# PSUM in eight one-bank tiles read by halves, sums of tile pairs copied from bank to bank, and a held-back channel sum in a Hymba-style layer

## The chip, the cores and the metric

The kernel runs on one core of a Trainium2 chip. The time is the device time of one execution in microseconds; the number that counts is the median over several runs.

## What is computed

One layer works on x of 1024 tokens and 1024 channels. Cut to what matters:

```python
h = rmsnorm(x, norm_g) * (1 + scale) + shift          # shift, scale, gate = silu(c) @ mod_w + mod_b
cv, cg, cs, lx, ls = split(h @ w_in)                  # five times 1024 channels
v = cv * sigmoid(cg)
v = causal_depthwise_conv(v, dw_w, dw_b)              # 31 taps
v = silu(layernorm(v, cln_g, cln_b))                  # over the channels
y_conv = (v @ pw2_w + pw2_b) * silu(cs)
xs = causal_depthwise_conv(lx, sc_w, sc_b)            # 4 taps
r = sigmoid(per head: xs @ wr + br); i = sigmoid(per head: xs @ wi + bi)
log_a = -8 * r * softplus(-lam)
hs = scan: h_t = exp(log_a) h_(t-1) + sqrt(1 - exp(2 log_a)) * (i * xs)
y_lru = hs * silu(ls)
x = x + (1 + gate) * (concat(y_conv, y_lru) @ w_out)
return rmsnorm(x, final_g)
```

## The kernel before

Everything is held with channels on 128 partitions and the 1024 tokens (T) along the free dimension; H is 512, half of them. A product in full precision is made of three matmuls: both operands are split into a high and a low part (`whi`, `wlo`; `uh`, `ul`), and high by high, high by low and low by high are added in PSUM. ScalarE casts the high part (L325), VectorE or GpSimd subtracts to get the low one (L352).

The work runs in this order. A first group of tiles, then 36 tiles `ps4` to `ps39` of the input projection (`mm_k`, L468: for each k both column halves), in the order of the list ORDER. Between them stand eight gates of the RG-LRU (`gates`, L1148): 12 matmuls each on `xsh`, `xsl`, the split result of the short convolution `xs`, with a low part that VectorE makes last. What is done with a finished tile is in `evac_in` (L1106): sigmoid, product, silu, short convolution. The 31-tap convolution is done on VectorE in two one-bank PSUM sums `cacc`, `caccs` for five of the eight channel tiles; for tiles 1, 3 and 5 ScalarE makes the products (`cq`, `co`) and DMAs issued by GpSimd add them up (`es`, `oo`). When a convolution is done, `c0` to `c7` are added up in `csum` (`conv_sum`, L1084): seven adds, the first six on GpSimd and the last on VectorE, in the order of SUMS, each when its operand is there.

Then come the tiles `ps40` to `ps47` of the output projection on the lru half. In between, the layer norm (L1178): the mean by a matmul on `csum` (L1184), subtractions, squares, their sums (L673), a spread of the inverse deviation over the partitions (`lnbc`, L679), multiplications, silu. Then `pw2` in four pairs of tiles and the conv half of the output projection: tile 6 on its own (`out`, L651), three pairs, tile 7. A pair (`pair_products`, L576 to L645) uses seven products of Strassen's scheme as Winograd wrote it (L590), 12 matmuls of 128x512 each, on sums of weight quarters (`rawpw`, `rawout`, split to `h12`, `l12`, `h34`, `l34`) and sums of token and channel quarters (`T1` to `T4`, `vt`, `vu`, `yt`, `yu`). Two two-bank tiles `pa`, `pb` take the products; ScalarE copies `pa` to SBUF (`e`), VectorE adds `pb` to it (`epw`, `eout`), and the readers take the sum of `e` and the rest of the tile. At the end stands the final norm by column pieces (`norm`, L1341) and the stores, issued by SyncE (L376) and ScalarE.

The order on each engine is fixed before the run by the class Plan: every operation has an engine, an estimated cost and a priority (n is the number of the tile in the order), operations it depends on, and buffers; a list scheduler picks for each engine the operation with the lowest priority that is ready in its model. Buffers come from pools (47 of [128, 1024] in SBUF; in PSUM three tiles of two banks and two of one); the next user of a buffer waits for the last reader of the one before. Each engine works through its own queue in that fixed order, so an operation that waits holds up all that stand behind it on its engine. DMAs are issued from the queues of SyncE, GpSimd and ScalarE.

Of the kernel before, what the change touches and what calls it, by code (L numbers as in the profile page):

```python
# [9 lines left out]
F32 = mybir.dt.float32  # L10
# [38 lines left out]
QGATES = ((2, 5), (3, 0), (3, 2), (3, 2))  # L49
OUT_A, OUT_P, OUT_Z = (6,), (0, 1, 2), (7,)  # L50
# [6 lines left out]
SUMS = (2, 6, 1, 4, 3, 0, 5, 7)  # L57
# [42 lines left out]
class Plan:  # L100
# [23 lines left out]
    def op(self, eng, cost, emit, prio, r=(), w=(), table=None, after=(), reserve=0,  # L124
# [28 lines left out]
        o.psum = [(b, any(k[0] is b for k in w)) for b in o.bufs if b.pool in ("mm", "acc")]  # L153
# [127 lines left out]
def hymba_layer(ctx: ExitStack, tc: tile.TileContext, xT, vecs, mod_w, w_first, w_in,  # L281
# [10 lines left out]
    psum = ctx.enter_context(tc.tile_pool(name="psum", bufs=3, space=bass.MemoryType.PSUM))  # L292
    psacc = ctx.enter_context(tc.tile_pool(name="psacc", bufs=2, space=bass.MemoryType.PSUM))
# [7 lines left out]
    pools["mm"] = (psum, "mm", [P, T], 3)  # L301
    pools["acc"] = (psacc, "acc", [P, H], 2)
# [35 lines left out]
    def in_psum(r):  # L338
        return any((k[0] if isinstance(k, tuple) else k).pool in ("mm", "acc") for k in r
                   if isinstance(k[0] if isinstance(k, tuple) else k, Buf))  # L340
# [39 lines left out]

    def part(b, a, e):
        return lambda: b()[:, a:e]

    def halves(b, a, e):
        return [(b, i) for i in range(b.parts) if i * (T // b.parts) < e
                and a < (i + 1) * (T // b.parts)]
# [75 lines left out]
    def mm_k(prio, ps, s, xh, xl, k, cols, off=0, nk=KT, after=()):  # L462
        wh, wl = whi[s], wlo[s]

        def emit():
            for lhs, rhs, last in ((wh, xh, 0), (wh, xl, 0), (wl, xh, 1)):
                for a, b in cols:
                    pe.matmul(ps()[:, a - off:b - off], k3(lhs)()[:, k, :], rhs[k]()[:, a:b],  # L468
                              start=(k == 0 and lhs is wh and rhs is xh
                                     and (a - off) % H == 0),  # L470
                              stop=(k == nk - 1 and bool(last)), skip_group_check=True)
# [9 lines left out]

    def mm_tile(name, parts=2):
        return S.buf("mm", name, F32, parts)

    def acc_tile(name):
        return S.buf("acc", name, F32)

# [88 lines left out]
    def pair_products(name, n, w, sets, apart=0, plain=False):  # L576

        pa, pb = (S.buf("mm", f"p{z}{name}", F32) for z in "ab")
# [3 lines left out]
        def product(q, a, b, ps, start):  # L585
            (wh, wl), xs = w[a], sets[b]
            for j, (bh, bl) in enumerate(xs):
                def emit(j=j, bh=bh, bl=bl):
                    for lhs, rhs, z in ((wh, bh, 0), (wh, bl, 1), (wl, bh, 2)):
# [4 lines left out]
                         [ps[0]], columns=3 * H)  # L594
                if j == 0:
                    ops.append(o)
        product(0, "A11", "B11", (pa, 0), True)
        if plain:
            pc = acc_tile(f"pc{name}")
            ACT(pr, half(e, 0), half(pa, 0), "copy", H, r=[pa], w=[(e, 0)])  # L600
            product(1, "S4", "B22", (pc, 0), True)
            product(2, "A12", "B21", (pa, 0), False)
            product(3, "S1", "T1", (pa, 1), True)
            ACT(pr, half(e, 1), half(pa, 1), "copy", H, r=[pa], w=[(e, 1)])
            product(4, "S2", "T2", (pb, 0), True)
            product(5, "S3", "T3", (pb, 1), True)
            TT(pr, "DVE", e, e, pb, ALU.add, r=[e, pb], w=[e])
            product(6, "A22", "T4", (pb, 1), False)
            yield ops, e, {(0, 0): (half(pa, 0), pa), (0, 2): (pc, pc),
                           (1, 1): (half(e, 1), (e, 1)), (0, 1): (half(pa, 1), pa),  # L610
                           (1, 0): (half(pb, 1), pb)}
            return
        if apart:
            ACT(pr, half(e, 0), half(pa, 0), "copy", H, r=[pa], w=[(e, 0)])
            f = big_buf(f"f{name}")
        else:
            product(1, "S1", "T1", (pa, 1), True)
            ACT(pr, e, pa, "copy", r=[pa], w=[e])
        product(2, "S2", "T2", (pb, 0), True)
        product(3, "S3", "T3", (pb, 1), True)  # L620
        if apart:
            TT(pr, "DVE", half(e, 0), half(e, 0), half(pb, 0), ALU.add, H, r=[(e, 0), pb],
               w=[(e, 0)])
            ACT(pr, part(f, 0, H), half(pb, 1), "copy", H, r=[pb], w=[f])
        else:
            TT(pr, "DVE", e, e, pb, ALU.add, r=[e, pb], w=[e])
        product(4, "A12", "B21", (pa, 0), False)
        if apart:
            product(5, "A22", "T4", (pb, 1), False)
            yield ops, e, {(0, 0): (half(pa, 0), pa), (1, 0): (half(pb, 1), pb)}  # L630
            n += apart
            product(6, "S1", "T1", (pa, 1), True)
            ACT(pr, half(e, 1), half(pa, 1), "copy", H, r=[pa], w=[(e, 1)])
            TT(pr, "DVE", half(e, 1), half(e, 1), part(f, 0, H), ALU.add, H, r=[(e, 1), f],
               w=[(e, 1)])
            product(7, "S4", "B22", (pa, 1), False)
            yield ops, e, {(1, 1): (half(e, 1), (e, 1)), (0, 1): (half(pa, 1), pa)}
            return
        product(5, "S4", "B22", (pa, 1), False)
        product(6, "A22", "T4", (pb, 1), False)  # L640
        yield ops, e, {(0, 0): (half(pa, 0), pa), (1, 1): (half(e, 1), (e, 1)),
                       (0, 1): (half(pa, 1), pa), (1, 0): (half(pb, 1), pb)}

    def tail_mm(prio, ps, off, s, sets, k, a, e):
# [4 lines left out]
        def emit():  # L649
            for lhs, (rhs, i), last in ((wh, (bh, ih), 0), (wh, (bl, il), 0), (wl, (bh, ih), 1)):  # L650
                pe.matmul(ps()[:, a - off:e - off], k3(lhs)()[:, k, :],  # L651
# [8 lines left out]
    def rstd(prio, sqs, a, e, ps, o, after=(), warm=(), idle=None):  # L660
# [4 lines left out]
        wk = halves(ps, o, o + e - a)  # L665
# [5 lines left out]
        def stats(sq, k):  # L671
            for b in range(nb):
                pe.matmul(ps()[:, o + b:o + b + 1], sq()[:, a + b * P:a + b * P + P],  # L673
# [3 lines left out]
        def spread(ps=ps):  # L677
            for b in range(nb):
                pe.matmul(ps()[:, o + b * P:o + b * P + P],  # L679
                          rs()[:, b:b + 1].to_broadcast([P, P]), ident, start=True, stop=True)  # L680
# [5 lines left out]
        ACT(prio, lambda: sd()[:, :nb], lambda: ps()[:, o:o + nb], AF.Sqrt, nb, bias=eps_t,  # L686
# [13 lines left out]
    psf = [mm_tile(f"first{n}", 4) for n in range(3)] + [acc_tile("first3")]  # L700
    psb = acc_tile("token_stats")
# [4 lines left out]
    cs, ps_c = ctile("cs", KT), [mm_tile(f"c_row{z}") for z in (0, 1)]  # L706
# [29 lines left out]
    def fw_mm(prio, ps, i, xh, xl, k, cols, after=(), off=0, z=None):  # L736
# [5 lines left out]
        def emit():  # L742
            for lhs, rhs, last in terms:
                for a, b in cols:
                    pe.matmul(ps()[:, a - off:b - off], fw_part(lhs, k, i * P, i * P + P)(),  # L745
# [174 lines left out]
    psx = mm_tile("psbias", 2)  # L920
# [52 lines left out]
    def by_two(b, a, e):  # L973
        return lambda: b()[:, a:e].rearrange("p (m q) -> p q m", q=2)
# [22 lines left out]
    def conv_tile(i):  # L997
# [19 lines left out]
        if i in POOLED:  # L1017
# [6 lines left out]
        acc, acs = acc_tile(f"cacc{i}"), acc_tile(f"caccs{i}")  # L1024
        acc_e, acc_s = half(acc, 0), half(acs, 0)
        ACT(pr, acc_e, ev, AF.Identity, H, scale=w(0), bias=vec("dw_b", i), r=[vi, ("V", 1)],
            w=[acc], after=held[-1:])
        o = ACT(pr, acc_s, src_s, AF.Identity, H, scale=ws(0), bias=b2,
            r=[(ci, 0), ("V", 1), ("wsum", 0)], w=[acs])
        held.append(o)  # L1030
# [7 lines left out]
        TT(pr, "DVE", every(1), every(1), acc_e, ALU.subtract, H, r=[ci, acc], w=[ci])  # L1038
        ACT(pr, acc_s, od, AF.Copy, H, scale=w(1), r=[vi], w=[acs])
        for r in range(1, 15):  # L1040
# [3 lines left out]
        TT(pr, "DVE", cut(every(0), 1, H), cut(every(0), 1, H), cut(acc_s, 0, H - 1), ALU.add,  # L1044
           H - 1, r=[ci, acs], w=[ci])
# [59 lines left out]
    def evac_in(m, ps, n, b=None, rb=()):  # L1105
        pr = n + 0.5  # L1106
        kind, i = (m // KT) * KT, m % KT
        if kind == CG:
            sig[i] = big_buf(f"sig{i}")
            ACT(pr, sig[i], ps, AF.Sigmoid, r=[ps], w=[sig[i]])  # L1110
        elif kind == CV:
            sg = sig.pop(i)
            v[i] = big_buf(f"v{i}")
            TT(pr, "DVE", apart(v[i], 0, T), by_two(ps, 0, T), by_two(sg, 0, T), ALU.mult,
               r=[ps, sg], w=[v[i]])
        elif kind == CS:
            t = big_buf(f"scs{i}")
            ACT(pr, t, ps, AF.Silu, bias=b, r=[ps, *rb], w=[t])
            scs_d[i] = dram.tile([P, T], F32, tag=f"scs{i}", name=f"scsd{i}")
            DMA(pr, lambda: scs_d[i], t, FULL_BYTES, r=[t], w=[("scsd", i)])  # L1120
        elif kind == LS:
            sls[i] = big_buf(f"sls{i}")
            ACT(pr, sls[i], ps, AF.Silu, bias=b, r=[ps, *rb], w=[sls[i]])
        else:
# [6 lines left out]
            ACT(pr, xs, ps, AF.Identity, scale=w(0), bias=vec("sc_b", i), r=[ps], w=[xs])  # L1131
            for s in range(1, STAPS):
                STT(pr, part(xs, s, T), part(ps, 0, T - s), w(s), part(xs, s, T), ALU.mult,
                    ALU.add, T - s, r=[ps, xs], w=[xs])
# [3 lines left out]
    def gates(i, n):  # L1138
# [3 lines left out]
        for j, (dst, b) in enumerate(((r, "br"), (g, "bi"))):  # L1142
            ps = mm_tile(f"gate{i}_{j}")

            def emit(j=j, ps=ps):
                for lhs, rhs, st in ((hi, xh, 0), (hi, xl, 1), (lo, xh, 2)):
                    for c0, c1 in FULL:
                        pe.matmul(ps()[:, c0:c1], lhs()[:, j, :], rhs()[:, c0:c1],  # L1148
                                  start=st == 0, stop=st == 2)
            S.op("PE", 6 * 0.2267, emit, n + 0.01 * j, [hi, lo, xh, xl], [ps],  # L1150
                 columns=6 * H)
            ACT(n + 0.2, dst, ps, AF.Sigmoid, bias=vec(b, i), r=[ps], w=[dst])
# [25 lines left out]
    def layer_norm():  # L1178
        pr = 45
        mean = mm_tile("mean")  # L1180
# [282 lines left out]
```

## Time and profile before

| | |
|---|---|
| median of 3 runs | 744.27 us (743.26 to 744.53) |
| the profiled execution | 745.16 us |
| its span, first to last instruction | 743.3 us |
| TensorE busy, mean granted clock | 731.4 us (98%), 0.996 |
| VectorE busy | 630.0 us (85%) |
| ScalarE busy | 446.8 us (60%) |
| GpSimd busy | 157.7 us (21%) |

The time of the profiled execution holds 1.9 us outside its span. PE is TensorE's matmuls, PEld its weight loads, DVE is VectorE, ACT ScalarE, POOL GpSimd and SP SyncE. Rows of the chain and of the timeline give the start in us from the span's start, the length, the engine, the line and the tile; rows of groups give the busy time, the mean ns of one instruction, and the idle time ahead of them with what ended it. Rows of the windows give for each engine its busy time and the number of its instructions, then the granted TensorE clock, the busy share of the DMA engines and their GB/s.

### The profile page before, as it was taken

The page shows a single profiled execution, that of the slowest core. Times are in us where ns is not written, and L with a number is a line of the kernel's source. Part 1 is how long each engine was busy: PE and PEld are TensorE (multiplying, and loading weights), DVE is VectorE, ACT ScalarE, POOL GpSimd, SP SyncE. Part 2 cuts the span into 40 slices and gives each one's busy share as a digit, 9 for nine tenths or more (in the row PEclk, how much of TensorE's full clock was granted, in tenths as well). Part 3 has the DMA queues.
Part 4 walks back from the last instruction along what each step waited for, and adds up shares of the span by engine and source line. Part 5 has one row for each costly group of instructions (what it writes and reads, how often), then busy time and mean ns, then how long its engine had stood idle before and what let it go on. Part 6 is the DMA issues. An engine that isn't in the chain of part 4 may idle for free.

```text
span 743.3 us, 8920 instructions
## 1 busy us (share of the span) xinstructions
PE 731.4 (98%) x3314; PEld 607.4 (82%) x3314; DVE 630.0 (85%) x818; ACT 446.8 (60%) x560; POOL 157.7 (21%) x137
## 2 busy tenths in 40 slices
PE   9999999999999999999998999999999999999996
PEld 8888888887888888888887888878888888877886
DVE  6998999896899886887899868886998766999945
ACT  6650587758877969937838685734843224455422
POOL 0033022462443433432272110400000000000003
PEclk9999999999999999999999999999999999999999
DMA  9961025586899799699483445252433530623206
GB/s 335 407 217 57 0 100 121 140 171 148 183 244 242 144 220 229 144 223 195 106 169 70 116 97 167 74 181 102 155 113 98 187 113 1 223 73 126 88 1 227
DMA packets 37052, 111.59 MB, mean 150 GB/s; under 512 B 4112, under 2 KB 12816, under 8 KB 37008
## 3 DMA queue, kind: packets, MB, share of 16 engines
q1 hardware_dynamic: 23616, 75.97, 29.3%
q0 software_dynamic: 12528, 34.26, 25.4%
q10 hardware_dynamic: 864, 0.79, 0.3%
q8 instruction: 26, 0.43, 0.2%
q14 instruction: 18, 0.15, 0.1%
HBM read 64.16 MB, written 12.58 MB: 103 GB/s over the span
## 4 chain that ended last, share of the span: by engine, by line
PE 83%; DVE 12%; ACT 2%; issue 2%; DMA 1%; SPq 0%; DVEq 0%; ACTq 0%
PE ps L468 59%; PE first L745 5%; PE papw L590 4%; PE pbpw L590 3%; PE gate L1148 3%; PE pbout L590 2%; PE paout L590 2%; PE out L651 2%; DVE wlo L352 1%; DMA fraw<-in_w_first_dram 1%; DVE xs L344 1%; DVE fin L344 1%; PE late L745 1%; DVE yu L352 1%; DVE rawout L352 1%
## 5 line engine op out<-in xcount | busy, mean ns | idle before, releaser
L468 PE MATMUL ps<-uh,whi 128*128 128x512 f32 x576 | 177.5, 389 | 0.6 <-ACT sls L333 0.6
L468 PE MATMUL ps<-uh,wlo 128*128 128x512 f32 x576 | 177.8, 390 | 0.0
L468 PE MATMUL ps<-ul,whi 128*128 128x512 f32 x576 | 177.7, 390 | 0.0
L468 PEld LDWEIGHTS ps<-uh,whi 128*128 128x128 f32 x576 | 108.0, 188 | 23.4 <-ACT sls L333 1.1
L468 PEld LDWEIGHTS ps<-uh,wlo 128*128 128x128 f32 x576 | 108.4, 188 | 22.6
L468 PEld LDWEIGHTS ps<-ul,whi 128*128 128x128 f32 x576 | 108.2, 188 | 22.4
L325 ACT CAST whi<-raw 128x1024 fp32r<-128x1024 f32 x46 | 48.1, 1048 | 50.2 <-PE ps L468 34.9
L352 POOL TENSOR_TENSOR o<-fin,bc 128x256 f32<-128x256 f32 (+1 forms) x8 | 7.3, 945 | 259.2 <-ACT bc L325 259.2
L357 POOL DMA_DIRECT2D es<-cq x45 | 40.7, 913 | 99.0 <-ACT cq L333 68.6
L333 ACT ACT_TABLE_LOAD x45 | 57.7, 1283 | 4.4 <-DVE sp8h L366 2.9
L352 DVE TENSOR_TENSOR wlo<-raw,whi 128x1024 fp32r<-128x1024 f32 x36 | 49.3, 1371 | 8.4 <-ACT whi L325 8.3
L344 DVE SCALAR_TENSOR_TENSOR cacc<-v,V,cacc 128x511 f32<-128x511 f32 (+14 forms) x75 | 55.5, 740 | 0.2
L357 POOL DMA_DIRECT2D oo<-co x42 | 40.8, 1016 | 59.8 <-ACT co L333 23.6
L344 DVE SCALAR_TENSOR_TENSOR caccs<-v,V,caccs 128x511 f32<-128x511 f32 (+6 forms) x70 | 52.1, 744 | 1.3
L344 DVE SCALAR_TENSOR_TENSOR caccs<-c,wsum,caccs 128x511 f32<-128x511 f32 (+6 forms) x70 | 52.0, 742 | 0.7
L352 POOL TENSOR_TENSOR wlo<-raw,whi 128x1024 fp32r<-128x1024 f32 x10 | 24.9, 2501 | 111.6 <-ACT whi L325 111.6
L468 PE MATMUL ps<-yh,whi 128*128 128x512 f32 x128 | 40.0, 394 | 0.0
L468 PE MATMUL ps<-yl,whi 128*128 128x512 f32 x128 | 39.5, 389 | 0.0
L468 PE MATMUL ps<-yh,wlo 128*128 128x512 f32 x128 | 39.4, 389 | 0.0
L333 ACT ACTIVATE cq<-v,V 128x511 f32<-128x511 f32 (+14 forms) x45 | 31.8, 706 | 0.0
L344 DVE SCALAR_TENSOR_TENSOR xs<-ps,V,xs 128x1023 f32<-128x1023 f32 (+2 forms) x24 | 30.6, 1273 | 0.5 <-ACT xs L333 0.5
L333 ACT ACTIVATE cq<-c,wsum 128x512 f32<-128x512 f32 x42 | 29.8, 711 | 0.0
(334 smaller groups left out, 1491.4 us busy)
## 6 DMA issues: line engine op xcount, KB each, us to landing
raw<-in_w_in_dram SPq DMA_DIRECT2D x36, 512.0 KB, 4.6
modw<-in_mod_w_dram SPq DMA_DIRECT2D x24, 512.0 KB, 8.9
raw<-in_w_out_dram SPq DMA_DIRECT2D x10, 512.0 KB, 3.9
x<-in_xT_dram SPq DMA_DIRECT2D x8, 512.0 KB, 10.9
scsd<-scs SPq DMA_DIRECT2D x8, 512.0 KB, 3.5
acc<-in_xT_dram SPq DMA_DIRECT2D x8, 512.0 KB, 5.0
accd<-acc SPq DMA_DIRECT2D x8, 512.0 KB, 2.7
rawpw<-in_pw_dram SPq DMA_DIRECT2D x8, 512.0 KB, 3.5
```

Source lines behind the costliest of these rows:

```text
L325: act.copy(out(), in_())
L333: act.activation(out=out(), in_=in_(), func=func, **kw)
L344: dve.scalar_tensor_tensor(out=out(), in0=in0(), scalar=scalar, in1=in1(), op0=op0, op1=op1, accum_out=accum)
L352: lambda: e.tensor_tensor(out=out(), in0=a(), in1=b(), op=op), prio, r, w,
L357: return S.op("POOL", ISSUE, lambda: pool.dma_start(out(), a(), accum_op=ALU.add), prio, r, w, lag=RATE * n / T, after=after)
L468: pe.matmul(ps()[:, a - off:b - off], k3(lhs)()[:, k, :], rhs[k]()[:, a:b], start=(k == 0 and lhs is wh and rhs is xh and (a - off) % H == 0),
L590: pe.matmul(half(*ps)(), half(*lhs)()[:, j * P:j * P + P], half(*rhs)(), start=start and j == 0 and z == 0, stop=j == KT // 2 - 1 and z == ...
L651: pe.matmul(ps()[:, a - off:e - off], k3(lhs)()[:, k, :], rhs()[:, i * H + a % H:i * H + a % H + e - a], start=k == KORD[0] and lhs is wh ...
L745: pe.matmul(ps()[:, a - off:b - off], fw_part(lhs, k, i * P, i * P + P)(), rhs()[:, a:b], start=k == 0 and lhs is wh and rhs is xh, stop=k ...
L1148: pe.matmul(ps()[:, c0:c1], lhs()[:, j, :], rhs()[:, c0:c1], start=st == 0, stop=st == 2)
```

## The change

Three things change. First, PSUM is one pool of eight one-bank tiles; a wide tile is a `Two`, two banks. A wide tile runs through all k of its first half and then of its second (also `out6`), the gates are made half by half, and each reader of a wide tile works on one half at a time. Second, in a pair each product has a bank of its own: ScalarE copies the first product from `p1` to `u3`, TensorE adds S2T2 there, ScalarE copies that to `e`, TensorE adds S3T3, ScalarE copies that to `c21`, where A22T4 is added; S1T1 is copied from `p5` to `e`. VectorE's add into `e` and one step of each gated sum go. A12B21 comes earlier in the order, S3T3 later. Third, the GpSimd adds of `csum` wait for the first matmul of `ps36`, and the last one, on VectorE, takes `c5` in place of `c7`. In the convolutions on VectorE the two sums wait for the last readers of the two before them (`held`).

The diff, cut to its core (the removed body of `pair_products` stands in the listing above):

```diff
+PEARLY = (3,)
+CSUM = 36
...
-SUMS = (2, 6, 1, 4, 3, 0, 5, 7)
+SUMS = (2, 6, 1, 4, 3, 0, 7, 5)
...
-    pools["mm"] = (psum, "mm", [P, T], 3)
-    pools["acc"] = (psacc, "acc", [P, H], 2)
+    pools["bank"] = (psum, "bank", [P, H], 8)
...
+    class Two:
+        def __init__(self, name):
+            self.b = [bank(f"{name}_{z}") for z in (0, 1)]
...
+    def pair_products(name, n, w, sets, apart=0, plain=False, early=False):
+        p1, u3, p5, c21 = ((bank(f"{z}{name}"), 0) for z in ("pa", "pu", "pb", "pc"))
...
+        def copy(to, src):
+            ACT(pr, half(*to), half(*src), "copy", H, r=[src], w=[to])
+        direct = {(0, 0): (p1,), (1, 0): (c21,)}
+        summed = {(0, 1): (p5, (e, 1)), (1, 1): (u3, (e, 0))}
+        product(0, "A11", "B11", p1, True)
+        copy(u3, p1)
         if plain:
+            pc = (bank(f"pd{name}"), 0)
+            product(1, "S4", "B22", pc, True)
+            product(2, "A12", "B21", p1, False)
+            product(3, "S1", "T1", p5, True)
+            copy((e, 0), p5)
+            product(4, "S2", "T2", u3, False)
+            copy((e, 1), u3)
+            product(5, "S3", "T3", u3, False)
+            copy(c21, u3)
+            product(6, "A22", "T4", c21, False)
+            summed[0, 1] = (pc, (e, 0), (e, 1))
+            yield ops, direct | summed
             return
+        if early:
+            product(1, "S1", "T1", p5, True, (0, 1))
+            product(2, "S2", "T2", u3, False)
+            copy((e, 1), u3)
+            product(2.4, "S1", "T1", p5, False, (2, 3))
+            copy((e, 0), p5)
+            product(3, "S3", "T3", u3, False)
+            copy(c21, u3)
+            product(4, "A12", "B21", p1, False)
+        else:
+            if not apart:
+                product(1, "S1", "T1", p5, True)
+                copy((e, 0), p5)
+            product(2, "S2", "T2", u3, False)
+            copy((e, 1), u3)
+            product(3, "A12", "B21", p1, False)
+            product(4, "S3", "T3", u3, False)
+            copy(c21, u3)
         if apart:
+            product(5, "A22", "T4", c21, False)
+            yield ops, direct
             n += apart
+            product(6, "S1", "T1", p5, True)
+            copy((e, 0), p5)
+            product(7, "S4", "B22", p5, False)
+            yield ops, summed
             return
+        product(5, "S4", "B22", p5, False)
+        product(6, "A22", "T4", c21, False)
+        yield ops, direct | summed
...
-            a, eng = (c[SUMS[0]] if i == SUMS[1] else csum), "DVE" if i == SUMS[-1] else "POOL"
-            TT(1000 + 5 * i, eng, csum, a, c[i], ALU.add, r=[a, c[i]], w=[csum])
+            a, end = c[SUMS[0]] if i == SUMS[1] else csum, i == SUMS[-1]
+            TT(1000 + 5 * i, "DVE" if end else "POOL", csum, a, c[i], ALU.add, r=[a, c[i]],
+               w=[csum], after=[] if end else [started[CSUM]])
...
-            ACT(pr, sig[i], ps, AF.Sigmoid, r=[ps], w=[sig[i]])
+            sig[i] = big_buf(f"sig{i}", parts=2)
+            for a, e in FULL:
+                ACT(pr, part(sig[i], a, e), part(ps, a, e), AF.Sigmoid, H, r=halves(ps, a, e),
+                    w=halves(sig[i], a, e))
...
-        for k in range(KT):
-            o = mm_k(n, ps, s, xh, xl, k, FULL)
-            if k == 0:
-                started[n] = o
+        for ch in FULL:
+            for k in range(KT):
+                o = mm_k(n, ps, s, xh, xl, k, (ch,))
+                started.setdefault(n, o)
...
-                if two:
-                    STT(n + 1, to, half(e, 0), g, to, ALU.mult, ALU.add, H,
-                        r=tk + [(e, 0), ("gate1", m)], w=tk)
-                STT(n + 1, to, src, g, to, ALU.mult, ALU.add, H, r=tk + [key, ("gate1", m)],
-                    w=tk)
+                for x in parts:
+                    STT(n + 1, to, half(*x), g, to, ALU.mult, ALU.add, H,
+                        r=tk + [x, ("gate1", m)], w=tk)
```

More of the change, by code (lines that the diff above doesn't have):

```diff
@@ L593, in product @@
                 o = S.op("PE", 3 * (H + 32) / 2400, emit, n + 0.15 * q, [wh, wl, bh, bl],
-                         [ps[0]], columns=3 * H)
+                         [ps], columns=3 * H)
                 if j == 0:
                     ops.append(o)
-        product(0, "A11", "B11", (pa, 0), True)
-        if plain:
[L599 to L611, printed above, removed]
-            return
@@ L613, in pair_products @@
-        if apart:
[L614 to L626, printed above, removed]
@@ L1121, in evac_in @@
         elif kind == LS:
-            sls[i] = big_buf(f"sls{i}")
-            ACT(pr, sls[i], ps, AF.Silu, bias=b, r=[ps, *rb], w=[sls[i]])
+            sls[i] = big_buf(f"sls{i}", parts=2)
+            for a, e in FULL:
+                ACT(pr, part(sls[i], a, e), part(ps, a, e), AF.Silu, H, bias=b,
+                    r=halves(ps, a, e) + list(rb), w=halves(sls[i], a, e))
         else:
@@ L1142, in gates, with emit @@
         for j, (dst, b) in enumerate(((r, "br"), (g, "bi"))):
[L1143 to L1152, printed above, removed]
+            ps = Two(f"gate{i}_{j}")
+            for c0, c1 in FULL:
+                def emit(j=j, ps=part(ps, c0, c1), c0=c0, c1=c1):
+                    for lhs, rhs, st in ((hi, xh, 0), (hi, xl, 1), (lo, xh, 2)):
+                        pe.matmul(ps(), lhs()[:, j, :], rhs()[:, c0:c1], start=st == 0,
+                                  stop=st == 2)
+                S.op("PE", 3 * 0.2267, emit, n + 0.01 * j, [hi, lo, xh, xl], halves(ps, c0, c1),
+                     columns=3 * H)
+                ACT(n + 0.2, part(dst, c0, c1), part(ps, c0, c1), AF.Sigmoid, H, bias=vec(b, i),
+                    r=halves(ps, c0, c1), w=[dst])
         pr = n + 1.0
@@ L1194, in layer_norm @@
                 TT(pr, "DVE", ss, ss, q, ALU.add, r=[ss, q], w=[ss])
[L1195 removed]
+        bc = Two("lnbc")
         rstd(-1, [ss], 0, T, bc, 0)
         for t in range(KT):
[L1198 removed]
+            for a, b in FULL:
+                TT(pr, "DVE", part(c[t], a, b), part(c[t], a, b), part(bc, a, b), ALU.mult, H,
+                   r=halves(c[t], a, b) + halves(bc, a, b), w=halves(c[t], a, b))
             ACT(pr, c[t], c[t], AF.Silu, scale=vec("cln_g", t), bias=vec("cln_b", t), r=[c[t]],
```

161 lines of the change are left out of this document (79 added, 82 removed).

## The prediction

> **What bounds the kernel now.** I read the totals of the page first, then the chain that ended last, then the list of what TensorE waited for, and last the windows around each wait.
>
> ```profile
> span 743.3 us, 8920 instructions
> PE 731.4 (98%) x3314; PEld 607.4 (82%) x3314; DVE 630.0 (85%) x818; ACT 446.8 (60%) x560; POOL 157.7 (21%) x137
> ```
> TensorE is busy for 98% of the span. The chain of waits (start, length, what) shows whether the busy time can shrink:
>
> ```profile
> 233.55 54.40 PE ps L468 x240
> 395.04 1.20 PE gate L1148 x4
> 396.24 2.15 PE ps L468 x6
> 398.39 2.18 PE gate L1148 x6
> 454.97 2.72 PE gate L1148 x12
> 518.40 1.78 PE lnbc L679 x16
> 520.19 51.72 PE ps L468 x228
> 571.90 5.44 PE papw L590 x24
> 626.30 2.73 PE pbpw L590 x12
> 726.35 2.88 PE out L651 x24
> ```
> 240 `ps` matmuls in 54.40 us are 0.2267 us each, with a weight used for two halves in a row. 24 `papw` matmuls in 5.44 us are 0.2267 as well, with a new weight each time. So the order of halves costs TensorE nothing, and since the changed program issues the same number of matmuls on the same number of columns, only gaps and half-rate time can change. The gaps (total, times, longest):
>
> ```profile
> PE gate L1148 <- DVE xsl L352: 2.3, 2, 1.9
> PE pbout L590 <- DVE fin L344: 0.8, 1, 0.8
> PE paout L590 <- ACT eout L325: 0.7, 1, 0.7
> PE ps L468 <- ACT sls L333: 0.6, 1, 0.6
> ```
> Behind the 1.9 us wait, the windows show a clock (the column after POOL) that the other stages don't have:
>
> ```profile
> 396.24:400.57 4.33, 4.33 (x13) 3.40 (x13) 4.33 (x7) 1.52 (x2) 0.00 (x0) 0.61 0.79 195
> 520.00:572.00 52.00, 52.00 (x232) 43.04 (x231) 50.18 (x60) 30.48 (x35) 0.00 (x0) 1.00 0.31 110
> 629.00:685.00 56.00, 54.72 (x241) 44.65 (x239) 55.72 (x75) 27.77 (x38) 0.00 (x0) 1.00 0.37 129
> ```
> The six `ps` and six `gate` matmuls there took 2.15 + 2.18 us where 12 × 0.2267 is 2.72, so 1.6 us more went; the four before them took 1.20 for 0.91. The fifth gate's stall thus costs 1.9 + 0.3 + 1.6 = 3.8 us. With 0.4 (the other gate wait), 0.6, 0.7 and 0.8, **6.3 us** can be removed at most. The last of these rows also says that VectorE is full (55.72 of 56 us) where the two pair waits fall.
>
> The Trainium skill ("TensorE: Matmul & The Clock Gate", What's actually happening) lets the clock fall after an idle window of about 3.4 us, and calls the window free-running. By it a 1.9-us gap costs 1.9 us, and the sum below would be 1.9 us poorer; the rows show half rate after that gap, and the measurement decides.
>
> **Why the fifth gate is late.** VectorE's and GpSimd's rows before it:
>
> ```profile
> 368.37 3.45 DVE L344 SCALAR_TENSOR_TENSOR r<-a,r 128x1024 f32<-128x1024 f32 x1 [0.17 <-ACT r L333]
> 372.88 2.30 DVE L352 TENSOR_TENSOR wlo<-raw,whi 128x1024 fp32r<-128x1024 f32 x1
> 375.76 2.76 DVE L352 TENSOR_TENSOR xs<-xs,r 128x1024 f32<-128x1024 f32 x1
> 391.65 3.33 DVE L352 TENSOR_TENSOR xsl<-xs,xsh 128x1024 fp32r<-128x1024 f32 x1
> 396.21 1.21 DVE L352 TENSOR_TENSOR wlo<-raw,whi 128x1024 fp32r<-128x1024 f32 x1
> ```
> ```profile
> 374.65 2.78 POOL L352 TENSOR_TENSOR csum<-csum,c 128x1024 f32<-128x1024 f32 x1
> 389.02 4.88 POOL L352 TENSOR_TENSOR csum<-csum,c 128x1024 f32<-128x1024 f32 x2
> ```
> Undisturbed, such an operation takes 1.21 (last row). Beside `csum` on GpSimd four of them take 3.45, 2.30, 2.76 and 3.33: 2.2 + 1.1 + 1.5 + 2.1 = 6.9 us lost, the last 2.1 directly ahead of the gate.
>
> **The change, part by part.**
>
> *csum held.* GpSimd's adds now start with the first matmul of `ps36`, 96 matmuls (21.8 us) ahead of gate 7, so at 454.97 − 21.8 = 433.2 on before's clock. The fifth gate keeps none of the 6.9 us, against a wait of 1.9: **−3.8** (bounds −3.8 to 0). `c5`, which was the sixth sum, now comes last, on VectorE. Behind the waiting add stand, on GpSimd's queue, the accumulating transfers `es5` 12 to 15 and `oo5` 12 to 14 of the last pooled convolution:
>
> ```profile
> 437.51 0.86 POOL L357 DMA_DIRECT2D es<-cq  x1 [5.80 <-ACT cq L333]
> 444.40 0.89 POOL L357 DMA_DIRECT2D es<-cq  x1 [5.14 <-DMA es<-cq]
> 443.73 1.20 DVE L352 TENSOR_TENSOR xsl<-xs,xsh 128x1024 fp32r<-128x1024 f32 x1
> L352 POOL TENSOR_TENSOR csum<-csum,c 128x1024 f32<-128x1024 f32 x5 | 13.7, 2733 | 0.2
> 474.63 3.46 DVE L352 TENSOR_TENSOR yl<-sls,yh 128x1024 fp32r<-128x1024 f32 x3
> 481.43 3.48 DVE L352 TENSOR_TENSOR yl<-sls,yh 128x1024 fp32r<-128x1024 f32 x3
> 487.62 1.72 PE mean L1184 x4
> ```
> Six sums of 2.73 us and two issues of 0.87 put `es5` 13 at 451.4. It lands within 7 us (chained adds stand 6.9 us apart, 437.51 to 444.40), by 458.3, and ScalarE's `g7`, whose buffer it frees, could start at 457.3 (nine matmuls into the gate, and 0.3 for the last to drain): at most 1 us late. Two more adds at 6.9 and some 8 us for the copies and folds give `c5` near 480. The mean is scheduled 66 matmuls later than before, 487.62 + 15.0 = 502.6, so 20 us are spare: 0.
>
> `xsl` of gate 7 ended 10 us ahead of its gate (444.9 to 454.97). In the changed order VectorE has more to do ahead of it; summing its operations by pitch leaves 6 us. Taken 0, up to +1.
>
> The first half of `ps40` asks for `yl7` 21 matmuls (4.8 us) earlier, since it runs through all k before the second half. By the same sum `yl7` is done at 482.8 and asked for at 484.4. Taken **+0.2** (0 to +2).
>
> *Layer norm.* It starts 15 us later while `pw2` starts at the same matmul; 168 matmuls, 38.1 us, lie between `lnbc` and `pw2` instead of 51.72. Its subtractions and multiplications become halves:
>
> ```profile
> 531.61 0.68 DVE L352 TENSOR_TENSOR vu<-c 128x512 f32<-128x512 f32 x1
> 532.21 0.68 DVE L352 TENSOR_TENSOR vt<-c,c 128x512 f32<-128x512 f32 x1
> ```
> A half has a pitch of 0.60 (531.61 to 532.21), a whole one of 1.14 ((3.48 − 1.21) / 2 from the `yl` row): +0.06 per split. From the first product with `lnbc` to the last operand split VectorE has 47 × 0.60 + 13 × 1.14 + 7 × 0.65 (the half with a scalar, estimated from these two) = 47.6 us. That is more than 38.1, but the last operands are needed only inside the first pair, whose products are interleaved to suit; matched operand by operand, three of them (`B21`, `T1`, `T2`, fourth quarters) have 0.2 to 0.6 us to spare. Taken **+0.6** (0 to +3).
>
> *Banks and halves.* The 0.6 us for `sls` was a wait for a two-bank tile to come free; with a bank per half and eight of them it goes: **−0.6** (−0.6 to 0). By sums of VectorE's order the tight gates 0, 1, 5 and 6 have 0.5 to 4.3 us more from the end of their `ps` to the time they ask for `xsl`, but gate 1 comes with more VectorE work ahead of it, so its 0.4 stays: 0 (−0.4 to +0.5). ScalarE issues 61 more instructions, mostly two halves for a whole; I estimate 17 to 20 us of its time, spread over a run in which it is 60% busy: 0 where it doesn't stand between two products, which is next.
>
> *Pairs.* In each pair ScalarE copies `p1` to `u3` and `u3` to `c21`, and TensorE goes on there. The copies by themselves, and a cast that may stand ahead:
>
> ```profile
> 661.70 0.59 ACT L325 COPY eout<-paout 128x512 f32<-128x512 f32 x1
> L325 ACT CAST whi<-raw 128x1024 fp32r<-128x1024 f32 x46 | 48.1, 1048 | 50.2 <-PE ps L468 34.9 <-issue 13.3 <-ACT c L333 0.8
> L352 DVE TENSOR_TENSOR epw<-epw,pbpw 128x1024 f32<-128x1024 f32 x4 | 4.9, 1219 | 5.5 <-PE pbpw L590 5.5
> ```
> Between the end of a source and its dependent lie mostly 12 other matmuls (2.72 us), 9 (2.04) in the first pair and 6 (1.36) once in the last. A cast of 1.05 already running and a copy of 0.59 are 1.64: under 2.04, over 1.36. Seven pairs with two hand-offs: **+0.5** (0 to +7, where the copy stands behind a cast that itself waits for VectorE). Against that VectorE loses a whole add (1.22, the `epw` row) and a half gated sum per pair. From 629 us to the last `l34out` of the last pair its work is 61.0 us by pitches against 68.5: 7.5 us less where it was full, so `fin` and `eout` come earlier and their buffers too: **−1.5** (−1.5 to 0).
>
> The first half of `out6` needs every `yc` 18 to 21 matmuls (4.1 to 4.8 us) earlier than the interleaved halves did, and `S1` of the first out pair follows: by the same sums up to 0.7 us late. Taken **+0.3** (0 to +2).
>
> *Tail.* The spread of the first `finbc` comes 35 matmuls later in the order, some 4.5 us, and with it the first stores:
>
> ```profile
> 725.46 0.89 PE finbc L679 x8
> 727.16 12.62 SPq L376 DMA_DIRECT2D out_dram<-o  x18
> ```
> 18 stores took 12.62 us to issue, 0.70 each, up to 739.8 of 743.3. The products behind them on VectorE now follow the last `fin`: **+0.6** (0 to +2).
>
> Sum: −3.8 − 0.6 − 1.5 + 0.2 + 0.6 + 0.5 + 0.3 + 0.6 = **−3.7 us**. Against the profiled execution (745.16, its span 743.3 and 1.9 outside it, 0.9 above the median) that is 741.5, and **740.6** on the scale of the median, 744.27. Its own range runs from 738 (all 6.3 removed) to 742.5.
>
> **Rivals.**
>
> *The stall moves to gate 7 and `ps40`.* Six sums now run in one stretch while VectorE makes `xsl7`. At before's rate (6.9 us lost on five sums) they cost 8.3 against a margin of 6: a wait of 2.3, with 1.9 more for the clock as at the fifth gate. 740.6 + 4.2 = 744.8, no change. For it: every sum of before hit something. Against: much of VectorE's work there reads PSUM, and those rows were not stretched. The Trainium skill ("SBUF — State Buffer", SBUF: two separate sides) says that such operations and GpSimd's exclude each other for a whole instruction. By it alone the loss could reach 6 × 2.73 = 16.4, and the wait 10 us.
>
> *Slower: ScalarE between products.* Where VectorE is full, casts on ScalarE wait for it in order, and the copy to the next bank waits behind them. It decides once VectorE is 1.1 us late (2.72 − 1.64); at 3 us late each hand-off loses 1.9. Two hand-offs in two pairs are 7.6, so 748.2, and a gap of 1.9 may add the clock's share. For it: 55.72 of 56. Against: the 7.5 us that VectorE saves there.
>
> *It doesn't do what it says.* `eout` and `fin` wait for VectorE's work and not for banks; if that stays, and the copies cost 0.2 us of latency at 14 hand-offs, 1.5 + 2.8 take the gain: 744.9.
>
> **How the numbers follow.** Forecast 0.64 (nearly all faster), stall moved 0.12, slower by hand-offs 0.14, nothing gained 0.05, several added waits at their upper ends 0.05. About 0.2%, 1.5 us, is what a measurement of this kernel can tell from no change: faster 0.66, same 0.15, slower 0.19. The range takes the forecast down to 737.8 and reaches over the no-change cases to 745.5.
>
> **What would show it.** Right: no `gate <- xsl` wait of 1.9 us near 393 and a clock of 1.00 in that stage; the adds of `csum` in the 430s and 440s; no wait for `sls`; no add of `pb` into `e` on VectorE, and 629 to 685 less than full. Wrong: `papw`, `pupw` or `pcout` products waiting for ScalarE's copies by over 0.5 us each; `gate` or `ps` waits near 455 or 484; `pw2` starting late; or the last store later after the last matmul than now.

## The result, and the profile after

The changed kernel takes 752.0 us (751.4 to 754.0) where the kernel before takes 744.3: the ratio is 1.011, with a 95% interval of 1.009 to 1.013. It is slower by 7.7 us, where 3.7 us less were forecast.

The totals of the profiled execution of the changed kernel, and what TensorE waited for (us in total, times, longest):

```profile
span 750.5 us, 8997 instructions
PE 732.9 (98%) x3314; PEld 608.0 (81%) x3314; DVE 619.9 (83%) x858; ACT 466.0 (62%) x627; POOL 162.0 (22%) x137
```
```profile
PE gate L1165 <- DVE xsl L352: 5.1, 2, 3.3
PE pbout L590 <- DVE l34out L352: 1.1, 1, 1.1
PE finbc L684 <- DVE rs64.6_0_5849 L694: 0.4, 1, 0.4
PE puout L590 <- ACT puout L325: 0.2, 1, 0.2
```
VectorE has 10 us less work than before and ScalarE 19 us more. TensorE still waits for `xsl`, longer than before (5.1 us for 2.3), but not at the same gates. Both traces hold 3314 matmuls, so the start of the n-th in one can be held against the n-th in the other. The difference, after less before, changes at these places:

| place | change, us | forecast |
|---|---|---|
| the first weights, ahead of everything | -0.4 | - |
| gate 1 and the bank of `sls` | +0.3 | -0.6 |
| gate 5 | -3.8 | -3.8 |
| gate 6 | **+6.5** | 0 |
| gate 7, `ps40`, mean, layer norm, start of `pw2` | 0.0 | +0.8 |
| seven pairs, `out6` | +0.6 | -0.7 |
| last matmul groups, up to the last spread | +0.4 | |
| from the last spread to the end of the span | **+3.6** | +0.6 for both |
| sum | +7.2 | -3.7 |

Gate 5 did what was forecast. Two places took it back and more: gate 6 and the end. Gate 6, on VectorE and GpSimd of the changed kernel:

```profile
417.24 3.43 DVE L352 TENSOR_TENSOR wlo<-raw,whi 128x1024 fp32r<-128x1024 f32 x1
421.25 2.70 DVE L352 TENSOR_TENSOR xsl<-xs,xsh 128x1024 fp32r<-128x1024 f32 x1
```
```profile
416.82 2.75 POOL L352 TENSOR_TENSOR csum<-c,c 128x1024 f32<-128x1024 f32 x1
419.65 3.21 POOL L352 TENSOR_TENSOR csum<-csum,c 128x1024 f32<-128x1024 f32 x1
440.91 0.88 POOL L357 DMA_DIRECT2D es<-cq  x1 [18.05 <-ACT cq L333]
444.48 10.79 POOL L352 TENSOR_TENSOR csum<-csum,c 128x1024 f32<-128x1024 f32 x3
```
`ps36` comes after gate 6 in TensorE's order, and gate 6 begins at 420.3. Yet the first two sums run at 416.8 and 419.65: they don't wait for `ps36`. The `after` of the change ties them to `ps36` in the plan alone, where the tie decides their place in GpSimd's queue; the instruction itself waits for VectorE and for a DMA, and not for TensorE. On the chip GpSimd reached that place earlier than the plan thought, and the two sums took 2.2 us from `wlo` and 1.5 from `xsl` (against 1.21 each undisturbed), right ahead of a gate. These 3.7 us are the whole wait: the gate's first two starts, 420.30 and 424.00, lie 3.5 us further apart than two matmuls in a row. TensorE then ran at half clock, as it had behind gate 5:

```profile
424.00:430.00 6.00, 6.00 (x14) 4.75 (x15) 5.29 (x8) 2.64 (x4) 0.00 (x0) 0.50 0.00 0
```
14 matmuls in 6 us at a clock of 0.50, where 26 fit.

The last of the later sums stretched `xsl` of gate 7 as well, to 3.36 us, but that was over 1.0 us ahead of its gate.

The end: the last pair's first half is spread over the partitions (`finbc`) at 732.84, 6.85 us ahead of the last spread; before it was 10.7 us ahead (725.30 to 736.03). The stores follow it. First the two spreads of the kernel before, then those and the stores of the changed one:

```profile
725.30 1.05 PE L679 MATMUL finbc<-ident,rs62.35_0_5537 128*128 128x128 f32 x8
736.03 0.71 PE L679 MATMUL finbc<-ident,rs64.6_0_5681 128*128 128x128 f32 x4 [0.15 <-DVE rs64.6_0_5681 L688]
```
```profile
732.84 1.05 PE L684 MATMUL finbc<-ident,rs62.35_0_5762 128*128 128x128 f32 x8
739.69 0.71 PE L684 MATMUL finbc<-ident,rs64.6_0_5849 128*128 128x128 f32 x4 [0.44 <-DVE rs64.6_0_5849 L694]
735.33 12.15 SPq L376 DMA_DIRECT2D out_dram<-o  x18
```
18 stores leave SyncE's queue over 12.15 us, up to 747.5, and the span ends 3.0 us later. Before, they left over 12.62 us, up to 739.8, and the span ended 3.5 us later. In both kernels the queue of stores ends last. Against the last spread it now begins 4.5 us later (4.4 us ahead of it in place of 8.9), and the span ends 3.6 us later (10.8 us behind it in place of 7.2).

### The profile page after: what moved, and what is told of

The parts are those of the page before. It is cut to its first block, busy times and chain, and to the rows that moved or that the text cites. A ratio compares the mean times of both kernels' runs of the same rounds, so it can differ in the third digit from the quotient of the medians.

```text
span 750.5 us, 8997 instructions
## 1 busy us (share of the span) xinstructions
PE 732.9 (98%) x3314; PEld 608.0 (81%) x3314; DVE 619.9 (83%) x858; ACT 466.0 (62%) x627; POOL 162.0 (22%) x137
## 5 line engine op out<-in xcount | busy, mean ns | idle before, releaser
L480 PE MATMUL ps<-uh,whi 128*128 128x512 f32 x576 | 224.6, 390 | 0.0
L480 PE MATMUL ps<-ul,whi 128*128 128x512 f32 x576 | 224.5, 390 | 0.0
L480 PE MATMUL ps<-uh,wlo 128*128 128x512 f32 x576 | 224.4, 390 | 0.0
L352 DVE TENSOR_TENSOR wlo<-raw,whi 128x1024 fp32r<-128x1024 f32 x36 | 46.2, 1283 | 18.5 <-ACT whi L325 18.0
L480 PE MATMUL ps<-yh,whi 128*128 128x512 f32 x128 | 50.5, 394 | 0.0
L480 PE MATMUL ps<-yh,wlo 128*128 128x512 f32 x128 | 49.9, 390 | 0.0
L480 PE MATMUL ps<-yl,whi 128*128 128x512 f32 x128 | 49.8, 389 | 0.0
L344 DVE SCALAR_TENSOR_TENSOR xs<-ps,V,xs 128x512 f32<-128x512 f32 (+3 forms) x48 | 35.8, 746 | 3.0 <-ACT xs L333 2.9
## 6 DMA issues: line engine op xcount, KB each, us to landing
x<-in_xT_dram SPq DMA_DIRECT2D x8, 512.0 KB, 10.7
```

What stands on the lines that cost most here:

```text
L344: dve.scalar_tensor_tensor(out=out(), in0=in0(), scalar=scalar, in1=in1(), op0=op0, op1=op1, accum_out=accum)
L352: lambda: e.tensor_tensor(out=out(), in0=a(), in1=b(), op=op), prio, r, w,
L480: pe.matmul(part(ps, a - off, b - off)(), k3(lhs)()[:, k, :], rhs[k]()[:, a:b], start=(k == 0 and lhs is wh and rhs is xh and (a - off) % ...
```

## The experiments

The theory after this reading (A) is that the sums stall whatever gate they stand ahead of, since nothing but their place in the queue holds them, and (D) that the order of the last pair sets the end. Against A stands that the halved readers leave VectorE too late by themselves (B), against D that the end is longer through the halves of the last tiles (E).

### The sums two transfers later in GpSimd's queue

```diff
-CSUM = 36
+CSUM = 37
```


> The changed kernel with CSUM 37 instead of 36: GpSimd's first two sums then stand behind the transfers es5 12 and oo5 12 in its queue. Theory A (the hold is only a place in the order; in the changed kernel GpSimd reached the sums at 416.8 us, and they ran against wlo and xsl ahead of gate 6): the 3.5 us wait and the 3.0 us of half rate at gate 6 go, 752.0 - 6.5 = 745.5 us, and no sum starts before 435 us. Rival B (the half-by-half readers leave VectorE too late for gate 6 by themselves): a wait of 1.5 us or more stays at gate 6, 749 us or more. Rival C (the stall moves on to gate 7): gate 6 is clean, gate 7 waits 2 us or more, 748 us or more.

750.8 us (749.4 to 751.6). Gate 6 is clean, and the stall stands at gate 7 instead, 2.8 us with a clock of 0.77 over the 7 us behind it. What TensorE waited for, then VectorE and GpSimd ahead of gate 7 in this kernel:

```profile
PE gate L1165 <- DVE xsl L352: 2.8, 1, 2.8
```
```profile
444.72 0.72 DVE L344 SCALAR_TENSOR_TENSOR xs<-ps,V,xs 128x509 f32<-128x509 f32 x1
445.36 2.73 DVE L352 TENSOR_TENSOR sls<-sls,r 128x1024 f32<-128x1024 f32 x1
448.01 3.41 DVE L352 TENSOR_TENSOR wlo<-raw,whi 128x1024 fp32r<-128x1024 f32 x1
451.94 2.79 DVE L352 TENSOR_TENSOR xsl<-xs,xsh 128x1024 fp32r<-128x1024 f32 x1
```
```profile
443.20 3.81 POOL L352 TENSOR_TENSOR csum<-csum,c 128x1024 f32<-128x1024 f32 x1
447.57 9.39 POOL L352 TENSOR_TENSOR csum<-csum,c 128x1024 f32<-128x1024 f32 x3
```
Theory A is right that the sums cause the stall, and theory C that it moves with them; A's time of 745.5 us did not come. B falls here: nothing is left at gate 6. The row that reads PSUM (`xs<-ps`) keeps its 0.72 in the middle of the sums; those that read SBUF alone are at two to three times 1.21.

### Without the hold

```diff
-SUMS = (2, 6, 1, 4, 3, 0, 7, 5)
+SUMS = (2, 6, 1, 4, 3, 0, 5, 7)
...
-               w=[csum], after=[] if end else [started[CSUM]])
+               w=[csum])
```


> The changed kernel without the hold and with the old order of the sums. Theory A: the sums run near 368 to 395 us again as before, gate 5 waits again (about 3.8 us with the half rate, less if the halves give it slack), gate 6 doesn't: 752.0 - 6.5 + 3.8 = 749.3 us or a little less. Rival B: gate 6 still waits, 752 us or more.

747.1 us (745.9 to 751.7), 4.9 under the changed kernel. Gate 5 has no wait, against the expectation. Its `xsl` and the GpSimd operations around it:

```profile
391.62 1.22 DVE L352 TENSOR_TENSOR xsl<-xs,xsh 128x1024 fp32r<-128x1024 f32 x1
```
```profile
371.11 2.96 POOL L352 TENSOR_TENSOR csum<-csum,c 128x1024 f32<-128x1024 f32 x1
392.53 1.49 POOL L352 TENSOR_TENSOR c<-c,es 128x512 f32<-128x512 f32 x1 [3.94 <-ACT c L325]
397.66 5.75 POOL L352 TENSOR_TENSOR csum<-csum,c 128x1024 f32<-128x1024 f32 x2
```
The sums run at 364 to 374 and 398 to 403 us, on either side of `xsl`, which keeps its 1.22. In the kernel before two of them stood beside it, from 389.02. Here the folds of a convolution (`c<-c,es`), which stand ahead of these two in GpSimd's queue, come at 392.53 in place of 383.51, so the sums fall behind the gate. It is their place that frees gate 5, and not time that the halves give: `xsl` is over 0.7 us ahead of its gate, as in the changed kernel; in the kernel of the next experiment, without halves, it is 1.0 us. Gate 6 waits 0.8 us with no sum beside it, so B holds for that much. In this kernel the hold costs 4.9 us.

### The hold alone, in the kernel before

```diff
-SUMS = (2, 6, 1, 4, 3, 0, 5, 7)
+SUMS = (2, 6, 1, 4, 3, 0, 7, 5)
...
-            TT(1000 + 5 * i, eng, csum, a, c[i], ALU.add, r=[a, c[i]], w=[csum])
+            TT(1000 + 5 * i, eng, csum, a, c[i], ALU.add, r=[a, c[i]], w=[csum],
+               after=[] if eng == "DVE" else [started[36]])
```


> The kernel before with nothing but the hold of the sums (adds tied to the start of ps36 in the plan, c5 last). In its order the sums stand behind es5 14 and oo5 14, so they can't start before 437 us. Theory A: gate 5's 3.8 us go, nothing comes in their place: 740.5 us. Rival C: the sums meet gate 7 or make the mean late, 742 to 746 us.

741.3 us (741.0 to 741.9), a ratio to the kernel before of 0.995 (0.994 to 0.997): 2.8 us are won. The waits and the sums of this kernel:

```profile
PE ps L468 <- ACT sls L333: 0.9, 2, 0.6
PE gate L1149 <- DVE xsl L352: 0.3, 1, 0.3
```
```profile
428.30 2.71 POOL L352 TENSOR_TENSOR csum<-c,c 128x1024 f32<-128x1024 f32 x1
431.09 6.63 POOL L352 TENSOR_TENSOR csum<-csum,c 128x1024 f32<-128x1024 f32 x2
438.27 9.42 POOL L352 TENSOR_TENSOR csum<-csum,c 128x1024 f32<-128x1024 f32 x3
```
The same line of code puts the sums behind `es5` 14 here and behind `oo5` 11 in the changed kernel, because the plan around it is another. They start earlier than expected (428, not 437 us). One of them meets `xsl` of gate 7, which takes 2.50 us for 1.21 but is over 8.7 us ahead of its gate; no gate waits for a sum.

### The hold later: CSUM 38 and 39

```diff
-CSUM = 36
+CSUM = 38
```


> The changed kernel with CSUM 38: only the first sum can come ahead of gate 7, the others stand behind es5 14, whose product ScalarE makes after that gate. Theory A: gates 5, 6 and 7 are all clean, the 6.5 us go: 745.5 us. Rival C (a single sum is enough to hold xsl ahead of gate 7): 748 us or more. Rival F (the sums now end too late for the mean): a wait of 1 us or more at the mean near 503 us.

746.1 us (745.0 to 747.6). Gates 5, 6 and 7 are clean and the mean isn't late; 5.9 of the 6.5 us come back. The profiled execution has 1.8 us at gate 1, which is taken up below.

```diff
-CSUM = 36
+CSUM = 39
```


> The same with CSUM 39: no sum ahead of gate 7 at all, five of them behind es5 15. Theory A: 745.5 us. Rival F: the mean or the layer norm late by 1 to 5 us, 746.5 to 751 us.

754.2 us (753.5 to 756.5), the slowest of all. The mean has no wait, so F fails as it was put; the sums run against the `yl` of `ps40` instead. The waits, GpSimd and VectorE of this kernel:

```profile
PE ps L480 <- DVE yl L352: 6.5, 7, 1.7
```
```profile
467.43 16.33 POOL L352 TENSOR_TENSOR csum<-csum,c 128x1024 f32<-128x1024 f32 x5
```
```profile
471.41 13.43 DVE L352 TENSOR_TENSOR yl<-sls,yh 128x1024 fp32r<-128x1024 f32 x4
```
Four `yl` take 13.43 us, 3.36 each; undisturbed they are 1.22 (group row of the changed kernel: 1218 ns). With every `yl` each k of `ps40` waits: seven waits.

So the place of the sums alone moves the time over 746.1, 750.8, 752.0 and 754.2 us.

### The last pair as before

```diff
+        if apart:
+            e4 = big_buf(f"f{name}")
+            copy((e, 0), p1)
+            product(2, "S2", "T2", u3, True)
+            product(3, "S3", "T3", c21, True)
+            TT(pr, "DVE", half(e, 0), half(e, 0), half(*u3), ALU.add, H, r=[(e, 0), u3], w=[(e, 0)])
+            copy((e4, 0), c21)
+            product(4, "A12", "B21", p1, False)
+            product(5, "A22", "T4", c21, False)
+            yield ops, {(0, 0): (p1,), (1, 0): ((e, 0), c21)}
...
```


> The changed kernel with the last of the out pairs made as before (S2T2 and S3T3 in banks of their own, VectorE adds them into e), in one-bank tiles. Theory D (the chain p1, u3, c21 puts A22T4 behind S3T3, the first half of the final norm 4 us later, and the first stores with it): the first final spread is 3 to 4 us earlier relative to the last one and the 3.5 us at the end go, 748.5 us. Rival E (the end is longer because of the halved readers and the final tile, not because of the pair's order): no gain, 751.5 us or more.

746.2 us (744.4 to 749.2), 5.8 less. In part that is luck. Between the two profiled executions lie 7.2 us, and the last pair and the end make 4.5 of them (0.5, 0.4 and 3.5). Another 2.0 are at gate 1, which doesn't wait here, and 1.2 behind gate 6, where the gap between matmuls is 3.70 us again but only 3.4 us of half rate follow, for 6.1 in the changed kernel. The next run is the cleaner one, since the sums are out of the way too:

> CSUM 38 and the last out pair made as before. Theory A with theory D: both gains, 752.0 - 6.5 - 3.5 = 742.0 us, 740 where gate 1 has no wait. Rival E: 745 us.

741.7 us (739.9 to 744.5), 4.4 under CSUM 38 alone, and a ratio to the kernel before of 0.997 (0.995 to 0.998). The first spread, the last one and the stores of this kernel:

```profile
721.07 1.05 PE L701 MATMUL finbc<-ident,rs62.35_0_5720 128*128 128x128 f32 x8
731.80 0.71 PE L701 MATMUL finbc<-ident,rs64.6_0_5864 128*128 128x128 f32 x4 [0.15 <-DVE rs64.6_0_5864 L711]
722.94 13.55 SPq L376 DMA_DIRECT2D out_dram<-o  x18
```
The stores begin 8.9 us ahead of the last spread, as in the kernel before (4.4 in the changed one), and the span of 739.7 ends 7.9 us behind it (10.8). The profiles of all the kernels here say the same: with the last pair as before the span ends 7.2 to 7.9 us behind the last spread, halves or not, and with the new order 10.8 to 11.9. Theory D holds, E falls. Against the profile of CSUM 38 the last pair and the end make 4.4 us; 2.0 more between the two are gate 1, which waits there and not here.

### All pairs as before

The other six pairs too: the products S2T2 and S3T3 in `u3` and `c21` of their own, VectorE adds both into `e` in halves.

```diff
...
+        q = 4 if plain else 2
+        product(q, "S2", "T2", u3, True)
+        product(q + 1, "S3", "T3", c21, True)
+        for z, u in ((0, u3), (1, c21)):
+            TT(pr, "DVE", half(e, z), half(e, z), half(*u), ALU.add, H, r=[(e, z), u], w=[(e, z)])
...
+        product(4, "A12", "B21", p1, False)
+        product(5, "S4", "B22", p5, False)
+        product(6, "A22", "T4", c21, False)
+        yield ops, {(0, 0): (p1,), (1, 1): ((e, 1), (e, 0)), (0, 1): (p5, (e, 0)), (1, 0): (c21, (e, 0))}
```


> CSUM 38 and all seven pairs made as before (VectorE adds into e), in one-bank tiles with halves. Against the run before it, this is the worth of ScalarE's copies from bank to bank in the other six pairs. Theory G (VectorE's shorter work there buys no time, since the waits left in the pairs are for l34out and for hand-offs): equal within 1 us. Rival H (the copies do pay, as was forecast with 1.0 us): 1 us or more slower. Against the kernel before with the hold alone (741.3 us) it is the worth of banks and halves.

740.7 us (740.4 to 741.4), a ratio to the kernel before of 0.996 (0.994 to 0.997), the lowest median of all. What TensorE waited for in the pairs, here and in the run before it:

```profile
PE pbout L590 <- DVE l34out L352: 0.4, 1, 0.4
```
```profile
PE pbout L590 <- DVE l34out L352: 1.1, 1, 1.1
```
1.0 us lies between the medians, and the intervals of the two ratios overlap, so in the times a loss by the copies isn't shown; a gain by them is not there. H falls. The traces say more: from the first pair to the last spread the kernel without the copies is 1.5 us shorter. Two hand-offs of 0.3 us each are gone, and the wait for `l34out` costs 0.7 less. So G is right that VectorE's shorter work buys nothing, but the copies cost something.

Against the hold alone (741.3) 0.6 us lies between the medians, and the intervals overlap: a gain by banks and halves is not shown. It isn't excluded either. In the two profiles the kernel with halves is 3.0 us shorter behind the first weights, but it lost 2.4 us at them, where TensorE waited 2.0 us for their cast. The changed kernel has no such wait, so it seems to belong to the execution and not to the halves; no run here settles it.

### Gate 1

In the profiles of the changed kernel and of CSUM 38 gate 1 waits 1.8 us, in the other six with halves up to here it doesn't. VectorE and GpSimd there, in the changed kernel and then in the one with CSUM 38 and the last pair as before:

```profile
171.66 3.87 DVE L352 TENSOR_TENSOR xsl<-xs,xsh 128x1024 fp32r<-128x1024 f32 x1
```
```profile
171.74 2.70 POOL L352 TENSOR_TENSOR modw<-modw,sc 128x1024 f32<-128x1024 f32 x1
```
```profile
172.77 1.22 DVE L352 TENSOR_TENSOR xsl<-xs,xsh 128x1024 fp32r<-128x1024 f32 x1
```
```profile
174.11 2.71 POOL L352 TENSOR_TENSOR modw<-modw,sc 128x1024 f32<-128x1024 f32 x1
```
Here `xsl` is longer by 2.65 us, about the length of GpSimd's operation; where `xsl` is over first, it keeps its 1.22. Where `xsl` is under way already, `modw` is the one held up (3.42 us for 2.70 with CSUM 37). `modw` comes when its DMA, and that of the `es` ahead of it in GpSimd's queue, have landed, so its time is not the plan's. To test this, one product was moved to VectorE, some ten operations behind `xsl`:

```diff
-        dot(GDOT, n, 2 * KT + j)
+        dot("DVE" if j == 2 else GDOT, n + (2 if j == 2 else 0), 2 * KT + j)
```


> The changed kernel with CSUM 38, and the product modw18 of the gate vector, which GpSimd makes around 172 us when its DMA has landed, made by VectorE some ten operations behind xsl of gate 1. Theory J (the wait of 1.8 to 1.9 us at gate 1 in two of the profiles is xsl blocked behind modw18, and whether it comes depends on which of the two starts first by less than 0.1 us): no wait of over 0.5 us at gate 1, the runs lie closer together, 744.5 us at the median, 1 to 2 us under the run with CSUM 38 alone (746.1). Rival K (VectorE's own work is late for gate 1 because of the halves): a wait of 1 us or more at gate 1 stays, 746 us or more.

749.3 us (748.1 to 750.2).

> The same move of modw18 in the kernel with CSUM 38 and all pairs made as before. Theory J: like the run without the move where gate 1 had no wait, 740.0 us (739.5 to 740.7). Rival K: no change or worse, 740.7 to 742 us.

743.3 us (742.9 to 744.4, 11 runs), a ratio of 0.999 (0.998 to 1.000). Gate 1 has no wait in either; that much of J is right, and K's late VectorE is not there. That the runs lie closer together isn't shown: 1.5 us over 11 runs, where 4 without the move lay within 1.0. And both times are 2.6 to 3.2 us higher than without the move. The plan behind it came out another way again, and now GpSimd's last folds of `c5` run against VectorE's scan and `yl7`. The waits, VectorE and GpSimd of the second kernel:

```profile
PE ps L480 <- DVE yl L352: 2.8, 1, 2.8
```
```profile
477.37 3.40 DVE L1220 TENSOR_TENSOR_SCAN r<-a,xs 128x1024 f32<-128x1024 f32 x1
480.81 2.16 DVE L352 TENSOR_TENSOR sls<-sls,r 128x1024 f32<-128x1024 f32 x1
482.89 3.44 DVE L352 TENSOR_TENSOR yl<-sls,yh 128x1024 fp32r<-128x1024 f32 x2
```
```profile
476.31 2.32 POOL L352 TENSOR_TENSOR c<-c,es 128x512 f32<-128x512 f32 x1 [11.36 <-ACT c L325]
478.71 5.40 POOL L352 TENSOR_TENSOR c<-c,oo 128x512 f32<-128x512 f32 x2
```
What the move would bring without this second effect stays open.

## Why the prediction was wrong

**The hold.** The step that failed is "GpSimd's adds now start with the first matmul of `ps36`", at 433.2. They started at 416.8. I took a tie in the plan for a wait on the chip. The forecast had no cost at gate 6; it lost 6.5 us, 3.5 of wait and 3.0 of half rate. The rival "the stall moves" had the right mechanism and a price of 4.2 us, but the wrong gate, as it was worked out from that same start. Four positions of the sums, with the stall each time where they stood (gate 6, gate 7, `ps40`) or nowhere, show it.

**Gate 5.** −3.8 forecast and measured, the half-rate stretch included, and no sum stands beside its `xsl` any more, as forecast. But the second experiment shows that the changed kernel didn't need the hold for it: without it the two sums fall behind gate 5 by themselves. The trace of before could not tell this.

**The end.** A term of the wrong size: +0.6 (0 to 2) against 4.0 (0.4 and 3.6). The lateness was right (4.5 us; 4.3 measured: 10.7 less 6.85, plus the 0.4 by which the last spread itself is late). Its price was not: the quoted row, 18 stores up to 739.8 of 743.3, said already that SyncE's queue ends last, so a late start is mostly paid at the end (3.6 of 4.5 us). I had costed only the products on VectorE. The 0.70 us for each store was no cost of issuing either: in the kernel before an issue itself took 0.33 to 0.59 us, and for the rest of the 12.62 us the queue waited.

**The pairs.** −0.7 forecast with `out6`, +0.6 measured. The waits for `fin` and `eout` did go, but one for `l34out` came at the first out pair: 1.2 us against the 0 to 0.7 in the text. Together these waits gave 0.6 us of the 1.5 forecast. VectorE's saving did not open a hole; between 632 and 688 us it is as full as before:

```profile
632.00:688.00 56.00, 54.91 (x240) 44.56 (x239) 55.24 (x75) 35.05 (x50) 0.00 (x0) 1.00 0.39 137
```
Work that is spared there is filled by what stands behind in its order, and the piece asked for first need not be the one that gains. The hand-offs cost 0.3, 0.3 and 0.5 us at three places, 1.2 for the +0.5 forecast; the rival of slow hand-offs, 1.9 us each, did not come.

**Gate 1 and `sls`.** The bank of `sls` gave its 0.6. Gate 1 took it back in this execution, by an operation of GpSimd (`modw`) that I had not counted among those that meet `xsl`.

**Layer norm, gate 7 and `ps40`.** +0.8 forecast, 0 measured. The spare time was less than worked out, though: `c5` was ready at 498.9 and not near 480, 6 us ahead of the mean at 505.0, because GpSimd stood idle for 17 us until ScalarE made the copy for its folds. The 6 us worked out for gate 7 are what the profiles show where no sum meets its `xsl` (6.07 with CSUM 38); in the changed kernel the sums left 1.0 of them. The row of the folds:

```profile
494.44 1.79 POOL L352 TENSOR_TENSOR c<-c,es 128x512 f32<-128x512 f32 x1 [17.04 <-ACT c L325]
```

The Trainium skill ("SBUF — State Buffer", SBUF: two separate sides) says that GpSimd and a VectorE operation with two SBUF inputs get a shared pair of ports for a whole instruction, and that the other one blocks. The rows agree: 3.87 for 1.22 beside an operation of 2.70, and 0.72 to 0.75 for those that read PSUM. It is of operations such as `xsl` that the rule speaks in the forecast as well, not of those that read PSUM.

## What to carry to other kernels

A dependency that exists only in a scheduler's model fixes an order, not a time: look on the instruction for the wait before you give it one, and if there is none, ask when the queue really gets there. Where two engines exclude each other, moving one engine's work moves the stall; it is won only when the new place has no deadline behind it, and every change of the plan has to be looked at anew. At the end of a kernel, follow the queue that finishes last: most of what starts it later is paid (3.6 of 4.5 us here).

## What the runs showed of the hardware

The clock fell to half after each gap between matmul starts of 2.24 us (the first weights of the run with all pairs as before), 2.30 us (gate 5 before) and more, up to 3.70; it did not after those of 2.14 us at gate 1 in two executions, nor after any shorter one. How long it stayed low does not follow from the gap: 3.4 us after the 2.30 us in the kernel before, 6.1 us of matmuls after the 3.70 us in the changed one, and 3.4 us after the same 3.70 us in the run with the last pair as before. The Trainium skill ("TensorE: Matmul & The Clock Gate", What's actually happening) gives an idle window of about 3.4 us for it and calls the window free-running. Shorter gaps were enough here; whether the window's position makes the difference, these few cases don't settle.

Which of two operations goes first was decided by tenths of a microsecond at gate 1, through the landing of DMAs, and is worth 2 us of the time. The rows' starts alone don't tell which: `xsl` begins 0.08 us ahead of `modw` in the changed kernel and is held up, and 0.06 us ahead of it with CSUM 37 and isn't. An execution's start varies as well: the cast of the first weights held TensorE for 0.3 to 2.5 us in several of the profiles and not at all in others.
